# A bidirectional DeltaNet encoder layer: two products of the DeltaNet chain take float32 operands in place of float16 pairs

## The chip, the cores and the metric

The kernel runs on one core of a Trainium2 chip. The metric is device time in microseconds (us), as the median of several executions. Everything said of where the time goes comes from one profiled execution. The engines are named as in the profile: PE (TensorE) multiplies matrices, PEld is its loading of the stationary operand, DVE is VectorE, ACT is ScalarE, POOL is GpSimd and SP issues the DMA transfers.

## The reference

One layer of an encoder, applied to two requests of 4096 and 2048 tokens with shared weights, in float32. The input projection feeds three groups of heads: attention in a window of 128, a gated DeltaNet that runs over the sequence forwards and backwards, and attention on a memory of 256 tokens. Each is multiplied by a gate; one output projection and a layer norm follow. The part that the change touches is the DeltaNet's recurrence, here cut to its core (chunks of 64 tokens, 4 heads, keys and values 64 wide, one state S of 64x64 for each head):

```python
def gated_delta_chunked(q, k, v, g, beta):
    ...
    u = solve(v * beta[..., None])
    w = solve(k_beta * jnp.exp(g)[..., None])
    qk = jnp.einsum('...id,...jd->...ij', q, k) * decay
    q_dec = q * jnp.exp(g)[..., None]
    k_dec = k * jnp.exp(g[..., -1:] - g)[..., None]
    g_tot = jnp.exp(g[..., -1])

    def step(S, xs):
        u_c, w_c, qk_c, qd_c, kd_c, gt_c = xs
        v_new = u_c - jnp.einsum('...cd,...de->...ce', w_c, S)
        o_c = jnp.einsum('...cd,...de->...ce', qd_c, S) + jnp.einsum('...ij,...je->...ie', qk_c, v_new)
        S = S * gt_c[..., None, None] + jnp.einsum('...cd,...ce->...de', kd_c, v_new)
        return S, o_c
    ...

def deltanet_branch(q, k, v, a, b, conv_w, A_log, dt_bias, norm_g):
    ...
    o = gated_delta_chunked(qs, ks, vs, gs, bs)   # both directions
    o = o[0] + o[1][..., ::-1, :]
    o = o * lax.rsqrt(jnp.mean(o * o, -1, keepdims=True) + RMS_EPS) * norm_g.astype(f32)
```

## The kernel before

The tokens are cut into 48 tiles of 128 (two tiles make a pair). Where float32 accuracy is wanted from float16 products, a float32 value is held as two float16 values, high and low: `split` writes the high part on ACT and the remainder on DVE, and `mm3` multiplies two such pairs in three products (high x high, high x low, low x high).

The program has three stretches in time. In the first (to about 1300 us) every tile gets its layer norm, projections, convolution and window attention. In the second, the forward one (about 1420 to 2400 us), the DeltaNet runs forwards over the 48 tiles, and beside it PE does the projection of the gates and the memory attention (`gate_proj`: 72 products a tile, tile `psg`). In the third, the backward one (about 2400 us to the end), the DeltaNet runs backwards, and beside it PE does the output projection (`finish`: 48 products of 512 columns a tile, tiles `pso<-w2a,yT` and `pso<-w2b,yT`).

For the DeltaNet a tile goes through these steps, in either direction:

- `dn_prep` (in `dn_front`, two pairs at a time): the products of keys with keys and with queries (`psk`), times decays, give `n` (the matrix to be inverted) and `p` (what multiplies the tile's own new values; float32). `p` is split into `phl`.
- `dn_invert`: `n` goes to DRAM (`nd`) and comes back as blocks of 32 (`na`), which POOL inverts in 30 dependent steps of two operations (`tb`, `nb`) for two pairs together; the result goes out (`ud`) and comes back (`uc`).
- `dn_prep2`: the tile's values `v32`, its features `fmc`, and the keys `n32` are loaded; POOL multiplies the keys by their decay (`kc32`, shown as `kc<-n,egs`), and `kc32` is split into `kc`, each key written twice so that 128 columns are filled.
- `dn_level`: two blocks of 32 become one of 64 (`psy`, `psz`, giving `th`).
- `dn_chain`: the recurrence itself. `psr` is the product with the state's pair `shl`; then `vs` and `v` on DVE; `psx` with `th` (float32 operands, one half of the tile), a copy on ACT; `psb` with `n` (float32), an addition on DVE; `psx2` with `th` (float32, the other half), a copy on ACT. Now `v32` holds the tile's new values. They are split into `rx`; `pss` is the product of `kc` with `rx` (`mm3`, four heads) and makes the new state `sf`; its split `shl` is what the next tile waits for. `pso` is the product of the features with the old state and of `phl` with `rx` (`mm3`), the tile's outputs.

The profile calls these tiles by their program names with the numbers left out: `v32` is `v`, `psx2` is `psx`, and the products of `phl` and `rx` are `pso<-rx,phl`. Nearly all instructions are recorded by one line (L505), so tiles tell them apart.

The order of the instructions on each engine isn't that of the code: `Plan` collects all operations and puts them in order with a model of costs, several times over, and keeps the order whose modelled end is earliest. It does this once for the first stretch and once for the other two. On the chip each engine then goes through its list in that order. The plan's price of a PE product counts its columns and takes float32 fourfold:

```python
            return max(25.0, 0.4167 * n + 2.5) * (4 if mybir.dt.size(ins[0].dtype) == 4 else 1)
```

Buffers that set how far things can run ahead: `n` and `phl` hold three pairs in one pool and one pair in another (`kept_front`), `kc` and `rx` two tiles.

Of the kernel before, what the change touches and what calls it, by code (L numbers as in the profile page):

```python
# [9 lines left out]
F32 = mybir.dt.float32  # L10
# [540 lines left out]
def encoder(ctx: ExitStack, tc: tile.TileContext, A, outs):  # L551
# [315 lines left out]
    def dn_prep(pool, psp, dr, t, e, n):  # L867
# [14 lines left out]

        p = pool.tile([P, 4, P], F32, tag="p", name="p", bufs=1)
        for hp in range(2):
            hs = slice(2 * hp, 2 * hp + 2)
            psk = psp.tile([P, 2, 2, P], F32, tag="fr", name="psk", bufs=1)
            for h2 in range(2):
                h = 2 * hp + h2
                T.matmul(psk[:, :, h2], lhsT=fm[:, 2 * h + 1, :], rhs=fm[:, 2 * h:2 * h + 2, :],
                         start=True, stop=False)  # L890
                T.matmul(psk[:, :, h2], lhsT=ks[:, h, :], rhs=fm[:, 2 * h:2 * h + 2, :], start=False, stop=True)
            V.tensor_tensor(n[:, hs], psk[:, 1], e[:, hs], op=ALU.mult)
            V.scalar_tensor_tensor(p[:, hs], psk[:, 0], -(2.0 ** 10), e[:, hs], op0=ALU.mult, op1=ALU.mult)
        d["n"] = n
        phl = pool.tile([P, 2, 4, P], F16, tag="phl", name="phl", bufs=2 * PAIRS)
        split(None, phl[:, 0], phl[:, 1], p)
        d["phl"] = phl
        d["t"], d["dr"] = t, dr
        return d

    def dn_prep2(pool, d):
# [7 lines left out]
        Q.dma_start(out=n32, in_=dn_d[d["t"]])  # L909
        kc32 = pool.tile([P, 4, 64], F32, tag="kc32", name="kc32", bufs=1)  # L910
        G.tensor_tensor(kc32, n32, eg[:, 1].unsqueeze(2).to_broadcast([P, 4, 64]), op=ALU.mult)
        kc = pool.tile([P, 2, 4, 2, 64], F16, tag="kc", name="kc", bufs=2)
        split(None, kc[:, 0], kc[:, 1], kc32.unsqueeze(2).to_broadcast([P, 4, 2, 64]))
        d["kc"] = kc
# [96 lines left out]
    def dn_chain(pool, psp, dr, d):  # L1011

        sf, shl = state["f"], state["hl"]
        fm, th, kc, phl, v32, eg, n = d["fm"], d["th"], d["kc"], d["phl"], d["v"], d["eg"], d["n"]
        fa = slice(0, 64) if dr == 0 else slice(64, 128)
# [25 lines left out]
        S.activation(v32[fb], px2[fb], AF.Copy)  # L1041
        rx = pool.tile([P, 2, 4, 64], F16, tag="rx", name="rx", bufs=2)
        split(None, rx[:, 0], rx[:, 1], v32, scale=2.0 ** -7)

        pss = psp.tile([P, 512], F32, tag="ch", name="pss", bufs=1)
        ps_ = pss[:, 0:256].rearrange("p (h d) -> p h d", h=4)
        for h in range(4):
            mm3(ps_[:, h], tuple(kc[:, a, h].rearrange("p s d -> p (s d)") for a in range(2)),
                (rx[:, 0, h], rx[:, 1, h]))
        st = pool.tile([P, 4, 64], F32, tag="st_", name="st_", bufs=1)  # L1050
        G.tensor_tensor(st, sf, eg[:, 2].unsqueeze(2).to_broadcast([P, 4, 64]), op=ALU.mult)
        sf2 = pool.tile([P, 4, 64], F32, tag="sf", name="sf", bufs=2)
        V.scalar_tensor_tensor(sf2, ps_, -(2.0 ** -10), st, op0=ALU.mult, op1=ALU.add)
        shl2 = pool.tile([P, 2, 4, 64], F16, tag="shl", name="shl", bufs=2)
# [8 lines left out]
        for h in range(4):  # L1063
            mm3(po[:, 1, h], (phl[:, 0, h], phl[:, 1, h]), (rx[:, 0, h], rx[:, 1, h]))
        return po, eg[:, 0]
# [389 lines left out]
    def dn_back(pool, psp, dr, tiles, ds, emit_out):  # L1455
        for i, (t, d) in enumerate(zip(tiles, ds)):
            dn_level(pool, psp, dr, d)
            first = pos_of[t] == 0 if dr == 0 else pos_of[t] == lens[seq_of[t]] - 1
            if first:
# [4 lines left out]
             for m in range(4)]  # L1464
# [9 lines left out]
    kept_front = {"n": (pf, "n", 1), "phl": (pf, "phl", 2), "uc": (pf, "uc", 1)}  # L1474
    early = dict(kept_front, nb=(pf, "nb", 1), tb=(pf, "tb", 1), fm=(pa, "aphl", 2), ks=(pa, "oat", 2), cr=(pa, "raw", 4), p=(pa, "rawv", 2),
                 na=(gx, "x", 3))
# [111 lines left out]
    for k in range(EARLY):  # L1588
        if k % 2 == 0:
            xTe = pa.tile([P, 2, 16, P], F16, tag="xT", name="xT", bufs=2)  # L1590
        gate_proj(gorder[k], xTe[:, k % 2], pa, (("qktm", 2), ("cth", 1)))
    plan.keep([d[k] for d in fr[0] for k in ("n", "phl", "uc")])
    plan.keep([wa, wb] + [x for g in gated.values() for x in g])
# [223 lines left out]
```

## Time and profile before

| | us |
|---|---|
| median of 3 executions | 3229.03 (3227.76 to 3230.68) |
| the profiled execution, its own time | 3223.55 |
| its span, first to last instruction | 3221.8 |
| PE busy | 2833.5 (88%) |
| DVE busy | 2652.9 (82%) |
| ACT busy | 2179.3 (68%) |
| POOL busy | 1765.8 (55%) |

The span is 1.75 us shorter than that execution's own time, and that execution is 5.5 us below the median. Busy time of PE is an upper reading, since products are pipelined and a group's last one is counted to its modelled end. The kernel has no single engine that is full throughout, so shares of the whole span say little by themselves: a change has to be priced in the stretch in which it acts.

### The profile page before, as it was taken

What the parts mean: (1) busy time and instruction counts of PE and PEld (TensorE: products, weight loads), DVE (VectorE), ACT (ScalarE), POOL (GpSimd) and SP (SyncE); (2) the same over time, 40 slices, a digit from 0 to 9 for tenths busy, and PEclk for the clock granted to TensorE, in tenths of its full rate; (3) what the DMA queues carried; (4) which work ended last, traced back from release to release, by engine and by line L of the source; (5) the groups of instructions that cost most, each with busy time, mean ns of one, the idle gap of its engine ahead of it and who ended that gap; (6) DMA issues with size and microseconds to landing.
All of it is one profiled execution on the core that took longest, in us unless ns stands there. A gap on an engine that the chain in (4) does not pass through costs nothing.

```text
span 3221.8 us, 79556 instructions
## 1 busy us (share of the span) xinstructions
PE 2833.5 (88%) x28704; PEld 1889.5 (59%) x28704; DVE 2652.9 (82%) x6256; ACT 2179.3 (68%) x5623; POOL 1765.8 (55%) x2923
## 2 busy tenths in 40 slices
PE   5789887888988897778999999999998998898998
PEld 4666766667666675445565555665554554554544
DVE  8799877899999999678878787887778887887875
ACT  5677756777777776577777667776666666565543
POOL 5756444455565455535734253444538766867762
PEclk9899988999999998889999999999999999999999
DMA  7999999999999999899888887877798887777763
GB/s 220 260 228 233 221 225 229 240 236 214 228 210 226 207 227 254 206 224 197 189 182 203 188 200 160 174 175 164 159 218 209 195 189 183 190 185 178 187 170 114
DMA packets 1336900, 652.35 MB, mean 202 GB/s; under 512 B 1127728, under 2 KB 1261744, under 8 KB 1332280
## 3 DMA queue, kind: packets, MB, share of 16 engines
q1 hardware_dynamic: 1336504, 647.27, 87.5%
q8 instruction: 225, 3.69, 0.5%
q14 instruction: 171, 1.40, 0.1%
HBM read 227.54 MB, written 175.19 MB: 125 GB/s over the span
## 4 chain that ended last, share of the span: by engine, by line
PE 24%; DVE 24%; POOL 19%; DMA 13%; issue 8%; ACT 8%; SPq 3%; POOLq 0%; ACTq 0%; DVEq 0%
PE psg L505 8%; POOL nb L505 6%; POOL tb L505 5%; DVE acc L505 5%; PE pso L505 4%; PE psf L505 3%; SPq L505 3%; DMA apt<-aphl 3%; DVE lg L505 2%; DVE aphl L505 2%; PE psk L505 2%; DMA na<-nd 2%; PE psx L505 1%; ACT lg L505 1%; DMA uc<-ud 1%
## 5 line engine op out<-in xcount | busy, mean ns | idle before, releaser
L505 PEld LDWEIGHTS <-xT 128*128 128x128 f16 x5760 | 535.7, 99 | 381.4 <-issue 43.8
L505 PE MATMUL psf<-xT,w1f 128*128 128x256 f16 (+1 forms) x3600 | 443.2, 276 | 13.3 <-DVE vtm L505 7.8
L505 PE MATMUL psg<-w2a,xT 128*128 128x512 f16 (+1 forms) x2304 | 435.5, 330 | 6.4 <-DVE qtm L505 4.4
L505 PEld LDWEIGHTS <-w1f 128*128 128x128 f16 x3600 | 341.0, 101 | 56.6 <-DVE vtm L505 7.2
L505 POOL TENSOR_TENSOR nb<-nb,tb 128x30 f32<-128x30 f32 (+6 forms) x750 | 342.7, 457 | 48.7
L505 POOL TENSOR_TENSOR tb<-nb,na 128x30 f32<-128x30 f32 (+6 forms) x750 | 327.0, 436 | 48.4
L505 DVE SCALAR_TENSOR_TENSOR acc<-cb,cw,acc 128x256 f32<-128x256 f32 x576 | 326.1, 598 | 7.3 <-POOL cb L505 4.6
L505 ACT ACTIVATE lg<-lg,mx,scal 128x385 f32<-128x385 f32 (+1 forms) x384 | 263.8, 688 | 89.7 <-DVE mx L505 81.6
L505 PEld LDWEIGHTS <-yT 128*128 128x128 f16 x2304 | 201.2, 98 | 193.2 <-issue 9.9
L505 PE MATMUL pso<-w2b,yT 128*128 128x512 f16 x1152 | 297.4, 385 | 0.0
L505 PE MATMUL pso<-w2a,yT 128*128 128x512 f16 x1152 | 291.5, 381 | 1.4 <-DMA yT<-yhl 1.4
L505 PE MATMUL pslg<-kfm,qfm 128*128 128x128 f16 x2240 | 197.3, 230 | 108.3 <-DVE mx L505 105.1
L505 PEld LDWEIGHTS <-qfm 128*128 128x128 f16 x2624 | 201.4, 102 | 154.3 <-issue 127.3
L505 PE MATMUL psg<-w2b,xT 128*128 128x512 f16 x1152 | 290.2, 384 | 0.0
L505 PE MATMUL psq<-w1t,xT 128*128 128x512 f16 x1152 | 283.2, 383 | 2.5 <-ACT cb L505 2.5
L505 POOL TENSOR_TENSOR x<-x,grow 128x256 f32<-128x256 f32 x208 | 189.1, 925 | 128.9 <-ACT x L505 117.4
L505 DVE TENSOR_TENSOR aphl<-lg,aphl 128x768 f16<-128x768 f32 (+1 forms) x192 | 201.5, 1049 | 56.2 <-ACT aphl L505 56.0
L505 POOL TENSOR_TENSOR n<-raw 128x256 f32<-128x256 f16 x96 | 79.6, 840 | 245.6 <-DMA raw<-cfh 113.1
L505 DVE CUSTOM_DVE_ANT_0 lg<-pslg,bias 128x385 f32<-128x385 f32 (+1 forms) x384 | 195.2, 540 | 22.8 <-ACT oat L505 10.8
L505 POOL TENSOR_TENSOR x<-x,brow 128x256 f32<-128x256 f32 x208 | 193.9, 949 | 0.0
L505 ACT ACTIVATE aphl<-lg 128x768 f16<-128x768 f32 (+1 forms) x192 | 156.4, 815 | 17.8 <-DMA apt<-aphl 15.9
L505 PE MATMUL psk<-w1t,xT 128*128 128x272 f16 x1152 | 157.9, 284 | 9.3 <-DVE qktm L505 9.2
(921 smaller groups left out, 6865.9 us busy)
## 6 DMA issues: line engine op xcount, KB each, us to landing
x<-x SPq DMA_DIRECT2D x48, 512.0 KB, 4.0
xT<-xT SPq DMA_DIRECT2D x24, 1024.0 KB, 5.8
xT<-xT SPq DMA_DIRECT2D x48, 512.0 KB, 4.7
r<-x SPq DMA_DIRECT2D x48, 512.0 KB, 4.1
out_dram<-r SPq DMA_DIRECT2D x48, 512.0 KB, 3.7
cr<-crow SPq DMA_DIRECT2D x47, 512.0 KB, 4.8
yhl<-yhl SPq DMA_DIRECT2D x48, 384.0 KB, 3.2
x<-in_x_prompt_dram SPq DMA_DIRECT2D x32, 512.0 KB, 4.9
```

The costliest lines, as they stand in the source:

```text
L505: getattr(self.eng[o["e"]], o["name"])(*o["args"], **o["kw"])
```

## The change

Three operands of the chain stay in float32. `p` is kept as it is (its own buffers have the slots that `phl` had, of the same size) and is not split; `v32` is used as it is and not split into `rx`; the decayed keys are written by ACT in float32, straight from the loaded keys with the decay as the scale, once for each head. The products of `pss`, and those of `pso` with the tile's own values, become one float32 product a head in place of three float16 products. Scale factors follow.

```diff
-        p = pool.tile([P, 4, P], F32, tag="p", name="p", bufs=1)
+        p = pool.tile([P, 4, P], F32, tag="phl", name="p", bufs=2 * PAIRS)
...
-            V.scalar_tensor_tensor(p[:, hs], psk[:, 0], -(2.0 ** 10), e[:, hs], op0=ALU.mult, op1=ALU.mult)
+            V.scalar_tensor_tensor(p[:, hs], psk[:, 0], -(2.0 ** 3), e[:, hs], op0=ALU.mult, op1=ALU.mult)
         d["n"] = n
-        phl = pool.tile([P, 2, 4, P], F16, tag="phl", name="phl", bufs=2 * PAIRS)
-        split(None, phl[:, 0], phl[:, 1], p)
-        d["phl"] = phl
+        d["p"] = p
...
-        kc32 = pool.tile([P, 4, 64], F32, tag="kc32", name="kc32", bufs=1)
-        G.tensor_tensor(kc32, n32, eg[:, 1].unsqueeze(2).to_broadcast([P, 4, 64]), op=ALU.mult)
-        kc = pool.tile([P, 2, 4, 2, 64], F16, tag="kc", name="kc", bufs=2)
-        split(None, kc[:, 0], kc[:, 1], kc32.unsqueeze(2).to_broadcast([P, 4, 2, 64]))
+        kc = pool.tile([P, 4, 2, 64], F32, tag="kc", name="kc", bufs=2)
+        for h in range(4):
+            S.activation(kc[:, h], n32[:, h].unsqueeze(1).to_broadcast([P, 2, 64]), AF.Copy, scale=eg[:, 1, h:h + 1])
...
-        rx = pool.tile([P, 2, 4, 64], F16, tag="rx", name="rx", bufs=2)
-        split(None, rx[:, 0], rx[:, 1], v32, scale=2.0 ** -7)
...
-            mm3(ps_[:, h], tuple(kc[:, a, h].rearrange("p s d -> p (s d)") for a in range(2)),
-                (rx[:, 0, h], rx[:, 1, h]))
+            T.matmul(ps_[:, h], lhsT=kc[:, h].rearrange("p s d -> p (s d)"), rhs=v32[:, h], start=True, stop=True)
...
-        V.scalar_tensor_tensor(sf2, ps_, -(2.0 ** -10), st, op0=ALU.mult, op1=ALU.add)
+        V.scalar_tensor_tensor(sf2, ps_, -(2.0 ** -17), st, op0=ALU.mult, op1=ALU.add)
...
-            mm3(po[:, 1, h], (phl[:, 0, h], phl[:, 1, h]), (rx[:, 0, h], rx[:, 1, h]))
+            T.matmul(po[:, 1, h], lhsT=p[:, h], rhs=v32[:, h], start=True, stop=True)
```

Since the operations differ, the plan makes another order for every engine. Two places show it.

On PE, in the backward stretch, before: the first product of `phl` and `rx` of a tile (`pso`) and the first of `kc` and `rx` (`pss`), which need the high parts alone. They stand among the output projection's products (`pso_24644`); the other eleven of each, a load and a product every time, follow some rows later.

```order
L505 LDWEIGHTS phl
L505 MATMUL pso<-rx,phl 128x64
L505 LDWEIGHTS kc
L505 MATMUL pss<-rx,kc 128x64
L505 LDWEIGHTS yT
L505 MATMUL pso_24644<-w2b,yT 128x512
```

And now, at a tile of the same stretch, between the output projection's products (`pso_24610`). A float32 product stands as one row with its load inside; "x4" are the four heads.

```order
L505 LDWEIGHTS yT
L505 MATMUL pso_24610<-w2a,yT 128x512
L505 MATMUL pso<-v_24623,p 128x64 x4
L505 MATMUL pss<-v_24623,kc 128x64 x4
L505 LDWEIGHTS yT
L505 MATMUL pso_24610<-w2a,yT 128x512
```

A tile's 24 products with 24 loads became eight rows. Of its four products with `p`, those that stand ahead of its last `pss` are 2.7 on average in the backward stretch and 1.7 in the forward one; of the twelve with `phl` it had been 8.5 and 6.2.

On DVE, in the backward stretch, from the addition in the middle of a tile's chain (`v<-psb`) to its new state (`sf<-pss`), before:

```order
L505 TENSOR_TENSOR v_25326<-psb,v_25326 64x256
L505 TENSOR_TENSOR yd<-yd,oss 128x256
L505 TENSOR_SCALAR ost<-ost,scal 128x1
L505 SCALAR_TENSOR_TENSOR r<-r,ost,w2b 128x1024
L505 TENSOR_TENSOR ydh<-yd,ydh 128x256
L505 TENSOR_TENSOR phl<-p,phl 128x512
L505 TENSOR_TENSOR cr<-cr,m_ge 128x512
L505 SCALAR_TENSOR_TENSOR rx<-v_25326,rx 128x256
L505 SCALAR_TENSOR_TENSOR r<-r,ost,w2b 128x1024
L505 TENSOR_TENSOR cr<-cr,m_ge 128x512 x2
L505 TENSOR_TENSOR ytl_21532<-psy,yth_21531 32x4x32
L505 TENSOR_TENSOR of<-of,pso 128x256
```

And now, at a tile there:

```order
L505 TENSOR_TENSOR v_25090<-psb,v_25090 64x256
L505 SCALAR_TENSOR_TENSOR sf<-pss,st__25109 128x256
L505 TENSOR_TENSOR ytl_21526<-psy,yth_21525 32x4x32
L505 TENSOR_TENSOR shl<-sf,shl 128x256
L505 TENSOR_TENSOR of<-of,pso 128x256
```

`rx` and `phl` are gone from DVE's list, and here no other work was put between `v` and `sf`: DVE stands at `sf` until PE has done the last `psx` and the tile's `pss`.

## Rows read from the trace of the kernel before

**Rows 1.** The stretches: busy time of each engine in the forward one and in the backward one. Columns: the stretch and its length in us, then busy us (and count of instructions) of PE, PEld, DVE, ACT and POOL, the granted share of the TensorE clock, the DMA engines' share and GB/s.

```profile
1420.00:2400.00 980.00, 916.23 (x9380) 582.45 (x9377) 784.80 (x1851) 701.95 (x1938) 462.21 (x1005) 0.98 0.82 185
2400.00:3222.00 822.00, 738.81 (x6766) 408.12 (x6764) 642.36 (x1475) 471.46 (x1308) 565.54 (x1009) 0.98 0.75 181
```

**Rows 2.** The chain of waits that ended last: the costliest lines' shares of the forward stretch, and of the backward one.

```profile
by line: PE psg L505 24.7%; POOL nb L505 8.0%; POOL tb L505 7.1%; issue 6.3%; PE psx L505 2.8%; DMA na<-nd 2.7%; DMA fm<-dst 2.6%; SPq L505 2.5%; PE psk L505 2.5%; DMA uc<-ud 2.1%; DVE mmx L505 1.7%; DMA cr<-crow 1.7%; ACT p L505 1.7%; PE p
by line: PE pso L505 14.5%; POOL nb L505 13.7%; POOL tb L505 11.5%; issue 6.9%; SPq L505 4.2%; DMA na<-nd 4.0%; POOL oss L505 3.3%; POOL of L505 3.0%; DMA uc<-ud 2.7%; DVE r L505 2.4%; PE psx L505 2.4%; DMA cr<-crow 2.1%; POOL ost L505 1.8%
```

**Rows 3.** What PE's products waited for from 1420 us to the end, longest first in total. Columns: who waited and for whom, us in total, times, the longest in us.

```profile
PE psx L505 <- DVE v L505: 27.0, 41, 1.9
PE psy L505 <- DVE tt L505: 20.7, 11, 3.4
PE psr L505 <- DVE shl L505: 16.1, 23, 2.0
PE psy L505 <- DVE of L505: 10.6, 8, 2.1
...
PE psr L505 <- ACT shl L505: 6.2, 8, 2.0
...
PE pso L505 <- DVE rx L505: 4.3, 8, 1.2
...
PE pss L505 <- ACT rx L505: 3.6, 4, 1.7
...
PE pss L505 <- DVE rx L505: 1.8, 2, 1.0
PE pso L505 <- ACT rx L505: 1.8, 2, 1.5
PE pss L505 <- DVE kc L505: 1.7, 1, 1.7
...
PE pss L505 <- ACT kc L505: 0.8, 1, 0.8
```

**Rows 4.** Groups of products and of loads of the stationary operand, whole span. Columns: line, engine, operation, tiles, shapes (for a load rows*columns; the moving operand's shape for a product), count | busy us, mean ns of one | idle us before, and who ended it.

```profile
L505 PE MATMUL psx<-v,th 64*64 64x64 f32 x1536 | 132.3, 226 | 31.8 <-DVE v L505 27.0 <-DVE ost L505 2.2 <-ACT th L505 0.9
L505 PEld LDWEIGHTS psx<-v,th 64*64 64x64 f32 x1536 | 106.0, 136 | 101.9 <-issue 52.8 <-DVE v L505 13.8 <-ACT th L505 8.8
L505 PE MATMUL pso<-rx,phl 128*128 128x64 f16 x1152 | 64.9, 193 | 6.5 <-DVE rx L505 4.5 <-ACT rx L505 1.8
L505 PE MATMUL pss<-rx,kc 128*128 128x64 f16 x1152 | 63.5, 193 | 8.5 <-ACT rx L505 3.6 <-DVE rx L505 1.8 <-DVE kc L505 1.7
L505 PEld LDWEIGHTS <-kc 128*128 128x128 f16 x1152 | 50.3, 98 | 22.0 <-issue 4.0 <-DVE kc L505 2.3 <-ACT kc L505 1.1
L505 PEld LDWEIGHTS <-gx 128*32 128x32 f16 x24 | 1.4, 96 | 0.4
```

**Rows 5.** Two places of the timeline, the loads of a float32 group and the products of two float16 groups that follow each other. Columns: start us, us from the first's start to the last's end, engine, line, operation, tiles, shapes, count.

```profile
1906.13 0.54 PEld L505 LDWEIGHTS psx<-v,th 64*64 64x64 f32 x8 [0.32 <-issue]
...
1912.55 0.48 PE L505 MATMUL pso<-rx,phl 128*128 128x64 f16 x11
1912.87 0.48 PE L505 MATMUL pss<-rx,kc 128*128 128x64 f16 x11
```

**Rows 6.** Groups on DVE, ACT and POOL, whole span: those that go, and ACT's copy of 128 elements with a scale. Columns as in Rows 4.

```profile
L505 DVE TENSOR_TENSOR kc<-kc,kc 128x512 f16<-128x512 f32 x96 | 73.0, 760 | 5.2 <-ACT kc L505 4.8
L505 ACT ACTIVATE th<-uc,scal 128x128 f32<-128x128 f32 x192 | 72.6, 392 | 0.9
L505 DVE TENSOR_TENSOR phl<-p,phl 128x512 f16<-128x512 f32 x96 | 69.7, 726 | 11.8 <-ACT phl L505 11.0
L505 POOL TENSOR_TENSOR kc<-n,egs 128x256 f32<-128x256 f32 x96 | 63.6, 663 | 100.2 <-DVE kc L505 60.9 <-DVE p L505 19.0 <-DMA n<-dn 7.9
L505 ACT ACTIVATE kc<-kc 128x512 f16<-128x512 f32 x96 | 60.5, 630 | 21.0 <-PE pss L505 10.2 <-POOL kc L505 8.7 <-POOL nb L505 1.5
L505 ACT ACTIVATE phl<-p 128x512 f16<-128x512 f32 x96 | 60.2, 627 | 6.0 <-DVE p L505 4.4
L505 DVE SCALAR_TENSOR_TENSOR rx<-v,rx 128x256 f16<-128x256 f32 x96 | 45.2, 471 | 11.6 <-ACT rx L505 11.1
L505 ACT ACTIVATE rx<-v 128x256 f16<-128x256 f32 x96 | 39.1, 407 | 1.0
```

**Rows 7.** The end of one tile's chain in the timeline of the backward stretch. Columns as in Rows 5; in brackets the engine's idle time before and who ended it.

```profile
2816.27 0.38 ACT L505 ACTIVATE v<-psx 64x256 f32<-64x256 f32 x1
...
2816.83 0.42 ACT L505 ACTIVATE rx<-v 128x256 f16<-128x256 f32 x1
...
2817.50 0.40 DVE L505 SCALAR_TENSOR_TENSOR rx<-v,rx 128x256 f16<-128x256 f32 x1
...
2818.14 0.48 PE L505 MATMUL pso<-rx,phl 128*128 128x64 f16 x11
...
2818.47 0.48 PE L505 MATMUL pss<-rx,kc 128*128 128x64 f16 x11
...
2818.99 0.42 DVE L505 SCALAR_TENSOR_TENSOR sf<-pss,st__25199 128x256 f32<-128x256 f32 x1 [0.76 <-PE pss L505]
```

**Rows 8.** The chain of waits, shares of a hundred us of the forward stretch (1900 to 2000 us).

```profile
by line: PE psg L505 19.3%; POOL nb L505 15.8%; POOL tb L505 13.3%; DMA na<-nd 5.8%; issue 5.7%; SPq L505 4.3%; DMA uc<-ud 3.9%; PE psk L505 3.2%; PE psx L505 3.0%; POOL kc L505 2.3%; DMA ud<-nb 2.0%; PE psb L505 1.8%; PE psmo L505 1.4%; PE
```

More of the change, by code (lines that the diff above doesn't have):

```diff
@@ L1013, in dn_chain @@
         sf, shl = state["f"], state["hl"]
-        fm, th, kc, phl, v32, eg, n = d["fm"], d["th"], d["kc"], d["phl"], d["v"], d["eg"], d["n"]
+        fm, th, kc, p, v32, eg, n = (d[k] for k in ("fm", "th", "kc", "p", "v", "eg", "n"))
         fa = slice(0, 64) if dr == 0 else slice(64, 128)
@@ L1474, in encoder @@
     kept_front = {"n": (pf, "n", 1), "phl": (pf, "phl", 2), "uc": (pf, "uc", 1)}
-    early = dict(kept_front, nb=(pf, "nb", 1), tb=(pf, "tb", 1), fm=(pa, "aphl", 2), ks=(pa, "oat", 2), cr=(pa, "raw", 4), p=(pa, "rawv", 2),
+    early = dict(kept_front, nb=(pf, "nb", 1), tb=(pf, "tb", 1), fm=(pa, "aphl", 2), ks=(pa, "oat", 2), cr=(pa, "raw", 4),
                  na=(gx, "x", 3))
@@ L1591, in encoder @@
         gate_proj(gorder[k], xTe[:, k % 2], pa, (("qktm", 2), ("cth", 1)))
-    plan.keep([d[k] for d in fr[0] for k in ("n", "phl", "uc")])
+    plan.keep([d[k] for d in fr[0] for k in ("n", "p", "uc")])
     plan.keep([wa, wb] + [x for g in gated.values() for x in g])
```

## The prediction

> **What bounds the kernel now.** The change acts only where the DeltaNet's chain runs, so I first read the two stretches apart [rows 1]. In the forward stretch PE is busy for 916 of 980 us (idle 64), in the backward one for 739 of 822 (idle 83). DVE follows with 785 and 642, ACT with 702 and 471, POOL with 462 and 566. PE is the fullest engine in both, at 93% and 90%.
>
> Next, the chain of waits [rows 2]. In the forward stretch it runs through the gates' products (`psg`, 24.7%) more than through anything else; POOL's inversion (`nb` and `tb`) has 15.1%. In the backward stretch POOL's operations in the row (`nb`, `tb`, `oss`, `of`, `ost`) have 33%, and the output projection (`pso`) 14.5%. So forwards PE's amount of work sets the pace; backwards it is shared between POOL's inversion and PE.
>
> Last, what PE waits for in its 147 us of idle time [rows 3]: results of DVE that belong to the chain, above all (`v` 27.0, `tt` 20.7, `shl` 16.1, `of` 10.6). The operands that go in this change account for 4.3 + 3.6 + 1.8 + 1.8 + 1.7 + 0.8 = 14.0 us.
>
> **PE.** A tile now has 12 + 12 float16 products for `pss` and `pso`, 1152 of each in all [rows 4]. In a row they follow each other every 0.029 us: eleven of `pso` take the 0.32 us from 1912.55 to 1912.87 [rows 5]. That is 24 x 0.029 = 0.70 us a tile.
>
> After it there are eight float32 products. The chip runs a float32 product in two passes: the code has 8 `psx` products a tile, 768 for 96 tiles and directions, and the trace has 1536 of them and 1536 loads [rows 4]. So 16 passes a tile. What a pass takes for a load of 128 columns no row shows, since the float32 operands of now have 64. Eight loads of that kind take 0.54 us, one 0.136 [rows 4, 5], so a pass comes every (0.54 - 0.136) / 7 = 0.058 us.
>
> The bounds: if columns don't matter to a load, 0.058 (float16 loads of 128 and of 32 columns take 98 and 96 ns [rows 4]); if the pass is as long as its load and that grows with the columns, 0.116. A float32 load of 64 columns takes 136 ns, longer than the 98 of a float16 load of 128, so float32 operands evidently load in another, slower way, and I place the value near the upper end, at 0.11: 16 x 0.11 = 1.76 us. PE's work grows by 1.06 us a tile, 102 us over 96 (bounds 0.23 x 96 = 22 and 1.16 x 96 = 111).
>
> The Trainium skill speaks against the change here: its page "TensorE: Matmul & The Clock Gate" says in "Weight-path perf modes — Fast Weight Load (FWL) and DoubleRow" that the fast load works for 128 columns and not for float32, and in "LDWEIGHTS (loading the stationary operand)" that a load takes its columns divided by 1.2 ns. By that rule a pass would be 107 ns and PE's added work, as an estimate, 16 x 0.107 - 0.70 = 1.01 us a tile, 97 us in all; by the rows' lower bound 22. For 64 columns the rule gives 53 ns, which the trace's 58 ns a pass agrees with; for 128 no run here shows it yet.
>
> The plan prices a float32 product of 64 columns at 4 x 29.2 = 117 ns, two passes of 58. If they take 110, PE runs 0.8 us a tile behind its plan, and what waits for `pss` or `pso` is late by that.
>
> **The other engines.** DVE loses the three remainders: 73.0 + 69.7 + 45.2 = 188 us [rows 6], nearly all in the two stretches, 13% of its 785 + 642 there. POOL loses the keys' decay, 63.6 us. ACT loses 60.5 + 60.2 + 39.1 = 160 us and gets four copies with a scale a tile; the nearest row (`th<-uc`, 128 elements, with a scale) has 392 ns, so 4 x 96 x 0.392 = 151 us: nothing gained, and one more thing in front of the chain's copies where the plan puts it there. The DMAs stay as they are. The buffers stay too: `p` has the slots of `phl`.
>
> **The chain's own length.** From the last copy of `v` (ends 2816.65) to `sf` (starts 2818.99) a tile takes 2.34 us now, through both halves of the split and eleven products of each kind [rows 7]. Afterwards it is a hand-off to PE, which I take as 0.2 us (from that copy's end to the split's start it is 0.18 here), perhaps 0.2 of a product under way, and 0.88 us for `pss`, about 1.4 with the drain; but with `p`'s four products ahead of `pss`, as the order has it for two thirds of them backwards and 42% forwards, up to 2.3. So the chain gets shorter by 0 to 0.9 us a tile, less than the removed split suggests, because the float32 passes take most of it back.
>
> **The sum.** PE's list gets 102 us longer; the question is how much of its 147 us of waiting goes. (a) The 14 us for `rx` and `kc` go. (b) Its four longest waits for DVE, 74 us in total [rows 3], shrink with a DVE that has 13% less to do; since such waits fall faster than load, I take a third, 25 us (bounds 10, by 13%, and 37, by half). (c) The waits for `shl`, 16.1 + 6.2 = 22.3 us, come right behind `pss`; where `pss` stands first, `p`'s products fill that time. Half: 11 us. (d) POOL's decay of the keys is on the chain of waits itself, 2.3% of a hundred us [rows 8]; over the stretches' 1802 us that would be 41. Half of it again, since the inversion's other waits stay: 20 us. Together 70 of 147.
>
> 102 - 70 = +32 us, against that execution's own 3223.55 us: 3255.6. The median lies 5.5 us above it, so 3261 us. The first stretch I leave as it is: it loses two tiles' splits of `p`, about 3 us of work beside 1300 us of other work, and its order changes throughout, which may move it by some us either way.
>
> **The rivals.**
>
> *PE's work is hidden and the backward stretch gets faster.* Its place is the backward stretch, its mechanism POOL's inversion, which holds a third of the chain there [rows 2]. Half of POOL's 63.6 us lies in it, 32 us; if that and 10 us of DVE waits come off the chain while PE's 51 us fit into its 83 idle ones, the stretch falls by 42. Forwards, 51 us meet only 64 idle ones [rows 1], and with half of (a) to (d) off, 16 remain. Together -26: 3203 us. It decides from the point where the backward stretch falls by more than the forward one rises. For it: POOL's share; against it: PE is at 90% there too.
>
> *A float32 load of 128 columns costs no more than one of 64.* Then PE's work grows by 22 us, and with the same 70 off it is -48: 3181 us. Against it is the 136 ns load.
>
> *PE's waits stay.* They belong to the chain's order, and the plan, which prices the passes too low, may put its waits elsewhere. Then only (a) is gained: 102 - 14 = +88, 3317 us.
>
> *Nothing to be measured.* Less than 0.2% either way, about 6.5 us, is what a measurement of this kernel can't tell from no change; the relief of DVE and POOL would just pay for the passes (3229 us).
>
> **How the numbers follow.** The forecast, about +7 to +65 us, gets 0.51; the waits that stay 0.12; nothing 0.11; the faster backward stretch 0.21; the cheap load 0.05. So slower 0.63, the same 0.11, faster 0.26. The range takes half of the faster backward stretch's cases and most of the staying waits': 3200 to 3313 us.
>
> **What would show it.** In the profile after: 1536 passes and loads each for `pss` and for `pso<-v,p`, and the stretch of eight passes, about 0.11 x 7 + 0.24 = 1.0 us against 0.48 for eleven now; with 0.058 it would be 0.65, and the load's duration would tell the same (some 190 ns against 136). DVE's busy time falls by about 188 us, POOL's by 64, ACT's by less than 20. PE's idle time in the two stretches falls from 147 to about 80 us and the stretches together grow by about 30, the forward one more than the backward. The prediction is wrong if the float32 passes come every 0.06 us, or if PE's idle time shrinks by more than 100 us, or if the first stretch moves by more than 10 us, which nothing in the sum provides for.

## The result

The changed kernel takes 3251.36 us (median; 3243.70 to 3255.10), beside 3228.40 for the kernel before on the same chip: a ratio of 1.0069, 95% interval 1.0047 to 1.0091, so 15 to 29 us slower. The profiled execution took 3248.76 us, with a span of 3247.0. The forecast had the median at 3261 us, +32; the sign is right, and the change costs +22. How much of the reasoning holds is what the experiments are about.

The stretches of the changed kernel, with the columns of [rows 1]:

```profile
1420.00:2400.00 980.00, 947.08 (x8941) 630.12 (x8940) 690.31 (x1679) 687.03 (x1963) 407.36 (x965) 0.99 0.80 182
2400.00:3247.00 847.00, 794.82 (x6534) 471.85 (x6532) 579.85 (x1376) 477.64 (x1396) 507.48 (x959) 0.98 0.75 180
```

PE is idle for 33 + 52 = 85 us now, where it was idle for 147 [rows 1], and busy for 87 us longer. DVE has 157 us less work in the two stretches and POOL 113, far more than its 64 us of decayed keys; what the rest is, the last section says.

The two new groups of products, their loads, and ACT's keys; columns as in [rows 4]:

```profile
L505 PE MATMUL pss<-v,kc 128*128 128x64 f32 x768 | 100.8, 272 | 0.2 <-ACT v L505 0.2
L505 PEld LDWEIGHTS pss<-v,kc 128*128 128x128 f32 x768 | 98.6, 193 | 6.6 <-ACT v L505 0.7
L505 ACT ACTIVATE kc<-n,egs 128x128 f32<-128x128 f32 x384 | 132.5, 394 | 36.9 <-PE pss L505 31.2 <-DMA n<-dn 4.5 <-issue 0.5
```

A load takes 193 ns on average, and 768 records are 384 products in two passes. The end of one tile's chain, to be held against [rows 7]:

```profile
2834.97 0.38 ACT L505 ACTIVATE v<-psx 64x256 f32<-64x256 f32 x1
...
2835.39 0.97 PEld L505 LDWEIGHTS pss<-v,kc 128*128 128x128 f32 x8 [0.71 <-ACT v L505]
2835.40 1.10 PE L505 MATMUL pss<-v,kc 128*128 128x64 f32 x8 [0.22 <-ACT v L505]
...
2836.34 1.06 PE L505 MATMUL pso<-v,p 128*128 128x64 f32 x8
...
2836.54 0.42 DVE L505 SCALAR_TENSOR_TENSOR sf<-pss,st__24971 128x256 f32<-128x256 f32 x1 [1.00 <-PE pss L505]
```

Eight passes take 2836.34 - 2835.40 = 0.94 us, and from the copy's end (2835.35) to `sf` it is 1.19 us, where the tile in [rows 7] took 2.34. That is one tile of each; over all 96 the median from the last copy to `sf` falls from 3.06 to 2.32 us. The chain did get shorter, and yet the kernel got slower.

PE's longest waits after, to be held against [rows 3]:

```profile
PE psx L505 <- DVE v L505: 13.2, 18, 2.9
PE psy L505 <- DVE tt L505: 12.6, 8, 3.3
PE psk L505 <- DVE p L505: 10.0, 9, 2.1
PE psr L505 <- DVE shl L505: 9.3, 14, 2.1
...
PE psr L505 <- ACT shl L505: 3.3, 6, 1.7
...
PE psy L505 <- DVE of L505: 0.8, 2, 0.4
```

The four waits for DVE that the forecast counted on (`v`, `tt`, `shl`, `of`) fell from 74.4 to 35.9 us. That looks like the forecast's term (b). Whether a lighter DVE did it isn't to be seen in a profile that changed in everything at once.

### The profile page after: what moved, and what is told of

Read it like the earlier page. It is cut to its first block, busy times and chain, and to the rows that moved or that the text cites. A ratio compares the mean times of both kernels' runs of the same rounds, so it can differ in the third digit from the quotient of the medians.

```text
span 3247.0 us, 77749 instructions
## 1 busy us (share of the span) xinstructions
PE 2914.7 (90%) x27936; PEld 1996.5 (61%) x27936; DVE 2488.3 (77%) x5968; ACT 2159.1 (66%) x5719; POOL 1657.8 (51%) x2827
## 5 line engine op out<-in xcount | busy, mean ns | idle before, releaser
L505 PE MATMUL psg<-w2a,xT 128*128 128x512 f16 (+1 forms) x2304 | 443.6, 330 | 4.2 <-DVE qtm L505 2.9
L505 POOL TENSOR_TENSOR nb<-nb,tb 128x30 f32<-128x30 f32 (+6 forms) x750 | 319.3, 426 | 49.7
L505 POOL TENSOR_TENSOR tb<-nb,na 128x30 f32<-128x30 f32 (+6 forms) x750 | 306.9, 409 | 50.3
L505 POOL TENSOR_TENSOR x<-x,grow 128x256 f32<-128x256 f32 x208 | 182.2, 892 | 144.3 <-ACT x L505 135.5
L505 PE MATMUL psov<-vtm,apt 128*128 128x64 f16 x3360 | 135.4, 196 | 46.1 <-DMA apt<-aphl 43.0
L505 PEld LDWEIGHTS <-apt 128*128 128x128 f16 x3360 | 125.6, 100 | 68.9 <-DMA apt<-aphl 56.1
```

Source lines behind the costliest of these rows:

```text
L505: getattr(self.eng[o["e"]], o["name"])(*o["args"], **o["kw"])
```

## Experiments

The theory is the forecast's: PE's added work comes whole, and a lighter DVE and POOL give some waits back. The rivals: PE's work is taken in by PE's own waits; or the new order of the instructions makes the difference. Ratios are to the kernel before on the same chip, with their 95% interval; a thousandth is 3.2 us. Where a run keeps every instruction at its place, the plan is given the old price for what was changed (those lines are left out below), and DVE, ACT and POOL go through the same lists as in the kernel that the run is held against.

### Less PE work after the change: 64 columns of `p`

```
-            T.matmul(po[:, 1, h], lhsT=p[:, h], rhs=v32[:, h], start=True, stop=True)
+            T.matmul(po[0:64, 1, h], lhsT=p[:, h, 0:64], rhs=v32[:, h], start=True, stop=True)
...
```

(DVE's two additions of this product take half the partitions)

> The changed kernel, with every instruction at its place, but the product of `p` with `v` loads only 64 of `p`'s 128 columns (the tile's own part of the output is left out for half of its tokens). In 8 of the 16 passes a tile the load then has the 64 columns that take 0.058 us a pass in the rows of before, where the trace after has 0.112: 8 x 0.054 x 96 = 41 us less work for PE, and not one operation less on another engine (DVE's additions have the same shape of half the partitions). Theory (the passes of 128 columns are what the change costs, and PE's amount of work sets the pace): 25 to 41 us below the changed kernel, 3210 to 3226 us. Rival (the new order of the work, or other waits, makes the difference, and PE's passes fill time in which it would wait): within 6 us of the changed kernel, 3245 to 3257 us.

3252.67 us, ratio 1.0059 (1.0038 to 1.0080): with the changed kernel's 1.0069 a difference of -3 us, uncertain by 10. The rival's number. The timeline of this run shows that the work did fall, though by far less than 41 us:

```profile
2424.92 0.68 PE L505 MATMUL pso<-v,p 128*64 128x64 f32 x8
...
2425.53 1.10 PE L505 MATMUL pss<-v,kc 128*128 128x64 f32 x8
...
2426.47 1.24 PE L505 MATMUL pso<-w2a,yT 128*128 128x512 f16 x5
```

The eight shorter passes take 0.61 us, the eight others 0.94 as in the changed kernel: 0.33 a tile, 32 us in all. That includes what PE pays for going on from loads of 64 columns to loads of 128; going over to 64 costs another 95 ns or so each time (last section), which leaves some 20 us less work. By the theory these should have shown as about 20 us; measured are 3, uncertain by 10, so they were worth less than that, but the test is weaker than was planned.

### Less DVE work before the change

```
-        split(None, rx[:, 0], rx[:, 1], v32, scale=2.0 ** -7)
+        S.activation(rx[:, 0], v32, AF.Copy, scale=2.0 ** -7)
...
+        V.scalar_tensor_tensor(rx[:, 1, 0], v32[:, 0], 2.0 ** -7, rx[:, 0, 0], op0=ALU.mult, op1=ALU.subtract)
...
-                (rx[:, 0, h], rx[:, 1, h]))
+                (rx[:, 0, h], rx[:, 1, 0]))
```

(and likewise for `phl` and `kc`)

> The kernel before, with every instruction at its place, but DVE makes the three remainders (of `kc`, `phl` and `rx`) for one head in four, and PE uses that one for all heads (the low parts of the other heads are left out). DVE has about 130 us less to do, PE, ACT and POOL the same. Theory (a lighter DVE shortens PE's waits, the terms (a) and (b) of the sum, and the chain): 15 to 35 us below the kernel before, 3193 to 3213 us, with PE's idle time in the two stretches falling from 147 by about the same. Rival (PE's own work is the bound and the relief of DVE is worth next to nothing, so that the saved waits come from somewhere else): 3220 to 3235 us.

3196.40 us, ratio 0.9888 (0.9859 to 0.9918): -36 us (-27 to -46), the theory's number. The stretches, in one row from 1420 us to the end, of the kernel before and of this one:

```profile
1420.00:3221.80 1801.80, 1655.04 (x16145) 990.57 (x16141) 1427.16 (x3326) 1173.41 (x3245) 1027.75 (x2013) 0.98 0.79 183
```

```profile
1420.00:3196.60 1776.60, 1652.45 (x16189) 993.38 (x16187) 1343.56 (x3330) 1173.06 (x3250) 982.24 (x2017) 0.98 0.80 186
```

DVE has 84 us less here (90 in the whole span, where 130 were expected), and PE's idle time falls from 146.8 to 124.2, its four waits for DVE from 74.4 to 50.6. POOL's busy time falls by 45 us although not one of its instructions changed. So the -36 us are not the price of DVE's work alone: POOL's shorter operations are in it, and so is the remainder of `rx` in the chain itself (284 ns on average, where it was 471).

### More DVE and POOL work after the change

```
+        V.tensor_tensor(pd, p, ks, op=ALU.subtract)
...
+        G.tensor_tensor(kc32, n32, eg[:, 1].unsqueeze(2).to_broadcast([P, 4, 64]), op=ALU.mult)
...
+        V.tensor_tensor(kd, kc32.unsqueeze(2).to_broadcast([P, 4, 2, 64]), d["fm"][:, 0:4].rearrange("p h (s d) -> p h s d", s=2), op=ALU.subtract)
...
+        V.scalar_tensor_tensor(rx, v32, 2.0 ** -7, fm[:, 0:4, 0:64], op0=ALU.mult, op1=ALU.subtract)
```

> The changed kernel, with DVE's three remainders (nothing reads them) and POOL's decay of the keys put back: DVE +188, POOL +64 us, PE and ACT as in the changed kernel; the plan orders it anew. Theory (the 60 to 80 us of PE's waits that the change won back came from DVE and POOL): 40 to 70 us above the changed kernel, 3290 to 3320 us, with the idle time of PE in the two stretches back at 125 to 155 us. Rival (PE, now busy for 95% of the stretches, hides them): 3245 to 3262 us.

3270.55 us, ratio 1.0118 (1.0089 to 1.0148): 16 us above the changed kernel, uncertain by some 12. Neither number, and PE's idle time is 108.5 us, between 85 and the 125 to 155 of the theory: the relief that the change gave is worth something, but well under the 40 to 70 us that the theory had.

```profile
1420.00:3268.10 1848.10, 1739.58 (x15379) 1093.77 (x15376) 1430.38 (x3325) 1155.40 (x3343) 1027.76 (x2018) 0.98 0.76 179
```

Two things differ from the run with less DVE work, though: the plan ordered this kernel anew, and nothing waits for the remainders here.

### Another price in the plan

```
-            return max(25.0, 0.4167 * n + 2.5) * (4 if mybir.dt.size(ins[0].dtype) == 4 else 1)
+            if mybir.dt.size(ins[0].dtype) == 4:
+                return 2.0 * max(58.0, 0.875 * self.free(ins[0]))
+            return max(25.0, 0.4167 * n + 2.5)
```

> The changed kernel, but the plan prices a float32 product by what its two passes take, 2 x 0.112 us for 128 columns and 2 x 0.058 for 64, where the changed kernel has 4 x 29.2 ns for both; the same instructions in another order. Theory (the price matters little, since PE works off its list anyway and its waits are mostly gone): 3240 to 3258 us. Rival (the plan lets PE run 0.8 us a tile behind, and what waits for it pays): 3230 us or less.

3301.12 us, ratio 1.0215 (1.0182 to 1.0248): 47 us above the changed kernel, which neither expected. The same instructions, planned with the passes' true duration, run slower. So an order alone can cost more than the change does.

### More PE work before the change

```
-            mm3(ps_[:, h], tuple(kc[:, a, h].rearrange("p s d -> p (s d)") for a in range(2)),
-                (rx[:, 0, h], rx[:, 1, h]))
+            mm3(pss[:, 64 * h:64 * (h + 3)].rearrange("p (k d) -> p k d", k=3),
+                tuple(kc[:, a, h].rearrange("p s d -> p (s d)") for a in range(2)),
+                tuple(rx[:, a, h].unsqueeze(1).to_broadcast([P, 3, 64]) for a in range(2)))
...
-            mm3(po[:, 1, h], (phl[:, 0, h], phl[:, 1, h]), (rx[:, 0, h], rx[:, 1, h]))
+            mm3(po[:, 1, h:4], (phl[:, 0, h], phl[:, 1, h]),
+                tuple(rx[:, a, h].unsqueeze(1).to_broadcast([P, 4 - h, 64]) for a in range(2)))
```

> The kernel before, with every instruction at its place on every engine, but the 24 float16 products of `pss` and `pso` a tile move more columns (192 each for `pss`, 256, 192, 128 and 64 for the four heads of `pso`; the surplus columns land where the next head's product overwrites them). By 1/2.4 ns a column, as the products of 512 columns in the trace show it (379 ns with their fill), PE gets 0.64 + 0.48 = 1.12 us more a tile, 107 us in all, which is what the float32 passes of the change cost (my 102), and no engine is relieved. Theory (in the forecast's sum PE's 102 us come whole and only a lighter DVE and POOL give waits back): 80 to 107 us above the kernel before, 3309 to 3336 us. Rival (PE's waits, 147 us in the two stretches, take a large part of the work in by themselves): 3250 to 3290 us, PE's idle time in the stretches then below 100 us.

3251.37 us, ratio 1.0064 (1.0040 to 1.0088): +21 us (+13 to +28) for 107 us of PE work. That is the rival, at the lower end of its range. The same row of this kernel, and then its longest waits of PE:

```profile
1420.00:3245.30 1825.30, 1737.25 (x16154) 1088.73 (x16150) 1429.31 (x3325) 1179.25 (x3245) 1034.07 (x2013) 0.99 0.77 181
```

```profile
PE psx L508 <- DVE v L508: 17.1, 31, 1.9
PE psy L508 <- DVE tt L508: 8.2, 8, 1.8
PE psr L508 <- DVE shl L508: 7.7, 17, 1.0
PE psy L508 <- DVE of L508: 6.1, 8, 1.1
```

PE's idle time is 88 us, nearly what the change left (85), and the four waits for DVE are down from 74.4 to 39.1 us, with DVE exactly as loaded as before (1429 us). While PE works longer, what it would have waited for gets ready. PE's added work alone is enough for the drop that I had put down to the lighter DVE.

PE's busy time grew by 82 us, not by 107. The granted clock is 0.99 in this row, where it was 0.98: by the trace's records PE ran at 1.2 GHz, the lower of its two levels, for 62 us of the two stretches before and for 24 here. Over whole executions the share is 0.963 to 0.970 here, 0.954 to 0.963 in the kernel before on the same chip. A clock that falls less often while PE has more to do is thus part of why the added work cost so little; as an estimate, 38 us less at half the speed save up to 19 us.

### The PE work of the change taken away

```
+        top = lambda x: x.bitcast(mybir.dt.bfloat16).rearrange("p (c two) -> p c two", two=2)[:, :, 1]
...
-            T.matmul(po[:, 1, h], lhsT=p[:, h], rhs=v32[:, h], start=True, stop=True)
+            T.matmul(po[:, 1, h], lhsT=top(p[:, h]), rhs=top(v32[:, h]), start=True, stop=True)
```

(and likewise for `pss`)

> The changed kernel, with every instruction at its place, but the eight float32 products a tile read only the upper halves of `kc`, `p` and `v` as bfloat16 (the lower 16 bits are left out): one pass each in place of two of 0.112 us. If a load of every second bfloat16 takes no longer than a float16 load (98 ns, hidden in part), PE has 1.2 to 1.5 us a tile less, 115 to 145 us in all; the other engines and the waits of every instruction are the same. Theory (PE's passes set the pace, and its waits come back in part): 55 to 110 us below the changed kernel, 3141 to 3196 us. Rival (after the change the chain and its order set the pace, not PE's work, as the 64-column loads hint): 3235 to 3257 us.

3224.23 us, ratio 0.9981 (0.9967 to 0.9995): 28 us below the changed kernel, between the two expectations. These products follow each other every 30 ns, so PE has 16 x 0.112 - 8 x 0.030 = 1.55 us a tile less, 149 us in all; again a microsecond of PE's work is worth 0.2. PE's idle time goes from 85 to 168 us, and the granted clock falls to 0.97 (96 us at 1.2 GHz, against 57 in the changed kernel):

```profile
1420.00:3222.80 1802.80, 1634.96 (x14692) 955.34 (x14689) 1268.66 (x3052) 1156.82 (x3353) 918.66 (x1923) 0.97 0.78 184
```

### What another order does

```
-    LAT = {"PE": 200.0, "DVE": 150.0, "ACT": 170.0, "POOL": 40.0, "SP": 0.0}
+    LAT = {"PE": 200.0, "DVE": 151.0, "ACT": 170.0, "POOL": 40.0, "SP": 0.0}
```

> The kernel before with the same instructions, ordered anew by a plan that takes DVE's latency as 151 instead of 150 ns. It shows what the order alone does. If an order is worth little: within 10 us of the kernel before, 3219 to 3239 us. If the difference of 22 us that was measured may be luck of the order: more than 15 us away, either side.

> The changed kernel with the same instructions, ordered anew by a plan that takes DVE's latency as 151 instead of 150 ns. If an order is worth little: within 10 us of the changed kernel, 3241 to 3261 us, and 15 to 30 us above the kernel before in its own second order. If the measured 22 us are luck of the order: more than 15 us away, either side.

The kernel before in its second order: 3231.03 us, ratio 0.9990 (0.9976 to 1.0004). The changed one in its second: 3240.43 us, ratio 1.0024 (1.0009 to 1.0038), so +8 us where the first order has +22: some 14 us less, uncertain by 9, and so between the two expectations. Slower it is in both, but by how much depends on luck of the order. The gain comes from the first stretch: the first state update (`sf`) starts at 1403.5 us in this order, at 1425.4 in the changed kernel's own, and at 1420.9 and 1417.3 in the two orders of the kernel before; what follows takes 1831.1 us, against 1821.6, 1800.9 and 1802.5 in the other three. In the stretches where the change acts it costs 20 to 30 us in either order. The first state update of the changed kernel, in its own order and in the second:

```profile
L505 DVE SCALAR_TENSOR_TENSOR sf<-pss,st__21584 x1: 425/425/425, 1425.4 to 1425.4; 128x256 f32<-128x256 f32 x1
```

```profile
L505 DVE SCALAR_TENSOR_TENSOR sf<-pss,st__21584 x1: 423/423/423, 1403.5 to 1403.5; 128x256 f32<-128x256 f32 x1
```

### Both edits of the kernel before at once

The diff is those of the second and the fifth experiment together.

> The kernel before, every instruction at its place, with both edits at once: PE's products of `pss` and `pso` with more columns (PE +107 us, alone +21) and DVE's three remainders for one head in four (DVE -90 us in the trace, alone -36; the low parts of the other heads are left out). Theory 1 (each engine's work has a price of its own, and they add up): 3230 + 21 - 36, that is 3207 to 3223 us. Theory 2 (with PE fuller a lighter DVE is worth little, which would explain why the change gains nothing from its lighter DVE and POOL): 3238 to 3255 us.

3220.19 us, ratio 0.9962 (0.9949 to 0.9976): -12 us, where the sum of the two gives -15. Theory 1: the prices add up, and a lighter DVE is worth as much with a full PE (-33) as without (-36).

```profile
1420.00:3221.50 1801.50, 1730.06 (x16191) 1088.35 (x16189) 1345.23 (x3331) 1183.88 (x3250) 992.64 (x2018) 1.00 0.79 183
```

This makes it a riddle why the change loses time. The changed kernel has about the same PE work as this one, and 75 us less on DVE and 78 less on POOL; yet its two stretches are 25 us longer (1827.0 against 1801.5), and PE waits 14 us longer in them. The other 12 us are PE's busy time, 1741.9 against 1730.1 for about the same work: the granted clock is 1.00 in the row above (11 us at 1.2 GHz), 0.99 and 0.98 in the changed kernel's (57 us).

### The change in halves

Only the state update; the diff is to the changed kernel, and puts the outputs' float16 pairs back:

```
+        phl = pool.tile([P, 2, 4, P], F16, tag="phl", name="phl", bufs=2 * PAIRS)
+        split(None, phl[:, 0], phl[:, 1], p)
...
+        split(None, rx[:, 0], rx[:, 1], v32, scale=2.0 ** -7)
...
-            T.matmul(po[:, 1, h], lhsT=p[:, h], rhs=v32[:, h], start=True, stop=True)
+            mm3(po[:, 1, h], (phl[:, 0, h], phl[:, 1, h]), (rx[:, 0, h], rx[:, 1, h]))
```

> One half of the change: the state update `pss` in float32 with `kc` from ScalarE, while the tile's own outputs stay with the float16 splits of `p` and `v`. PE +51, DVE -73 (of `kc`), POOL -64 us; `rx` and `phl` stay. At the prices per microsecond that the experiments so far give (PE 0.2, DVE 0.4 where PE is not full): +10 - 29 and something for POOL, 3195 to 3215 us. If relief is worth little once PE gets more work: 3232 to 3250 us.

Only the tile's own outputs; to the changed kernel again:

```
+        G.tensor_tensor(kc32, n32, eg[:, 1].unsqueeze(2).to_broadcast([P, 4, 64]), op=ALU.mult)
...
+        split(None, kc[:, 0], kc[:, 1], kc32.unsqueeze(2).to_broadcast([P, 4, 2, 64]))
...
+        split(None, rx[:, 0], rx[:, 1], v32, scale=2.0 ** -7)
...
-            T.matmul(ps_[:, h], lhsT=kc[:, h].rearrange("p s d -> p (s d)"), rhs=v32[:, h], start=True, stop=True)
+            mm3(ps_[:, h], tuple(kc[:, a, h].rearrange("p s d -> p (s d)") for a in range(2)),
+                (rx[:, 0, h], rx[:, 1, h]))
```

> The other half: the tile's own outputs in float32 from `p` and `v`, while `pss` keeps the float16 splits of `kc` and `rx`. PE +51, DVE -70, ACT -60 us; POOL and the chain's `rx` as before. At the prices so far: +10 - 28, 3205 to 3220 us. If relief is worth little once PE gets more work: 3235 to 3255 us.

The state update alone: 3227.11 us, ratio 0.9980 (0.9966 to 0.9994), -6 us, between the two expectations. The outputs alone: 3248.51 us, ratio 1.0045 (1.0029 to 1.0061), +15 us, as if relief were worth little. So the prices found in the order of before don't carry over to programs that the plan orders anew. In the outputs' half the first state update starts 14 us later than in the kernel before (1434.6 against 1420.9), which is half of the 27 us that separate the two profiled executions (the medians differ by 15): again the order of the first stretch, in which this half changes next to no work. The halves sum up to +9 us, about what the changed kernel shows in its second order.

### No remainders at all

```
-        split(None, phl[:, 0], phl[:, 1], p)
...
-        split(None, rx[:, 0], rx[:, 1], v32, scale=2.0 ** -7)
+        S.activation(rx, v32, AF.Copy, scale=2.0 ** -7)
...
-            mm3(po[:, 1, h], (phl[:, 0, h], phl[:, 1, h]), (rx[:, 0, h], rx[:, 1, h]))
+            T.matmul(po[:, 1, h], lhsT=p[:, h], rhs=rx[:, h], start=True, stop=True)
```

(and likewise for `kc` and `pss`)

> The kernel before without the low parts: `kc`, `p` and `v` are rounded to float16 and each head has one product for `pss` and one for `pso` (the remainders and their products are left out, `p` is written in float16 at once). DVE -188, PE -16 x 0.029 x 96 = -45, ACT -60 us, POOL as before; the plan orders it anew. With the prices so far (DVE 0.4, PE 0.2): -75 - 9, 3140 to 3160 us. If DVE's relief is worth only what lies on the chain itself (the remainder of `rx`, 0.3 to 0.5 us a tile, and the eleven products, 0.3): 3155 to 3190 us. If the order counts for more than either: 3190 us and up.

3176.04 us, ratio 0.9826 (0.9807 to 0.9845): -56 us, faster than both kernels, at float16's accuracy in these two products. That is in the range of the second expectation, by which relief counts for what lies on the chain; the order may have its part. It has the PE work of the run with upper halves and the same DVE (1276 against 1269 us), more POOL (984 against 919) and 28 us less ACT, and is 48 us faster. What sets the two apart is the order, planned for what runs here and for products of 117 ns there, and the way `kc` and `rx` are made: by POOL and one copy of ACT each here, by ACT's four copies and not at all there.

## Why the prediction was right, and where it was not

**PE's added work: right.** The row of eight passes lasts 1.10 us (forecast 1.0), passes follow each other every 0.112 us (median; forecast 0.11), and a load takes 193 ns (190): 16 x 0.112 - 0.70 = 1.09 us a tile, 105 us (102). By this the rival of the cheap load is out. The rule of the Trainium skill (page "TensorE: Matmul & The Clock Gate", section "LDWEIGHTS (loading the stationary operand)") gave 107 ns a pass, and the trace agrees within 5%; the load's own record is longer, 193 ns. Wrong was the count among the signs: there are 768 passes for `pss` and as many for `pso<-v,p`, 1536 together; the sum had the right 16 a tile. DVE's busy time fell by 165 us in the whole span (forecast 188), POOL's by 108 (64) and ACT's by 20 (less than 20).

**PE's idle time: right in size (85 us, forecast 80), wrong in cause.** The failed step is "102 - 70" as a sum of a cost that comes whole and of waits that a lighter DVE and POOL give back. With 107 us more work and no relief at all PE's idle time falls just as far, from 147 to 88. PE's work costs 0.2 us per us, in either kernel's order (+21 for 107, -28 for 149; the -3 for 20 doesn't speak against it). PE is the fullest engine at 93% and 90% [rows 1] and still its amount of work doesn't set the pace. So the term was about 20 us, not 102. Two more things in the 70 don't hold: the 16.1 us for `shl` stand in (b) and again in (c), about 5 us twice, and (d) is POOL's time on the chain of waits, taken off PE's idle time.

**(a) to (c):** the waits went, but PE's added work alone is enough for that. What a lighter DVE is worth in the kernel before is about what (b) said, in PE's idle time (-23 us), and more in the time (-36). The chain from the last copy to `sf` got shorter by 0.74 us in the median, within the forecast's 0 to 0.9.

**(d) POOL's decay of the keys: not seen in the time.** What POOL waited for from 1420 us on, before and after:

```profile
POOL nb L505 <- DMA na<-nd: 130.9, 37, 18.3
POOL kc L505 <- DVE kc L505: 60.9, 22, 8.8
POOL ost L505 <- DVE ost L505: 57.5, 17, 9.4
```

```profile
POOL nb L505 <- DMA na<-nd: 174.0, 40, 13.4
...
POOL ost L505 <- DVE ost L505: 122.5, 21, 11.3
```

Two waits grew by 43 + 65 = 108 us, and the 60.9 us for `kc` are gone. In all POOL is idle for 138 us more in the stretches, its 113 us less of work and the 25 us by which they got longer. The 2.3% of the chain of waits [rows 8] don't show up as a gain: POOL waits longer instead, for the blocks of the next inversion (`na`) and for DVE (`ost`). What the decay alone is worth no run shows.

**Where +22 us come from.** In the order of before, PE's 107 us more and DVE's 90 us less were worth -12 together, and the change takes off nearly twice as much on DVE. It lost 22 us, or 8 in its second order. So the forecast had PE's cost five times too high; it took 70 us off for the relief, where 33 to 36 were measured for about half of DVE's; and it lacked a loss of 20 to 35 us. That these come out near the measured number together is luck.

The traces show where much of the loss sits. The chain runs through four tiles, whose inverses (`th`) are made together, and then needs the inverses of the next four. From the 49th state update on there are 47 steps from one update's start to the next. The 36 inside the groups of four take 472 us now and took 546: the shorter chain gains 74 us. The 11 that lead into a new group take 349 us and took 265. In ten of these 11 the first copy of `v` starts within 1.5 us of the last copy to `th`, so the chain is waiting for the inverse, as it was before at these steps. With both edits in the order of before (the riddle above) it is 534 and 266 us, 800 together, against 821 now. One group after the change, and the same group before it: the first `n`, the last `sf` of the group two ahead, the last `th`, and the chain's first product with it.

```profile
2717.34 1.06 PE L505 MATMUL pso<-v,p 128*128 128x64 f32 x8
2717.54 0.42 DVE L505 SCALAR_TENSOR_TENSOR sf<-pss,st__24754 128x256 f32<-128x256 f32 x1 [0.16 <-PE pss L505]
...
2718.23 0.27 PE L505 MATMUL psk<-fm,ks 128*128 128x256 f16 x1
...
2718.54 0.42 DVE L505 TENSOR_TENSOR n<-psk,cr 128x256 f32<-128x256 f32 x1 [0.58 <-PE psk L505]
...
2815.19 0.56 ACT L505 ACTIVATE th<-psz 32x128 f32<-32x128 f32 x2 [1.05 <-PE psz L505]
...
2815.70 0.68 PE L505 MATMUL psx<-v,th 64*64 64x64 f32 x8
```

```profile
2690.86 0.42 DVE L505 TENSOR_TENSOR n<-psk,cr 128x256 f32<-128x256 f32 x1 [2.89 <-PE psk L505]
...
2712.16 0.42 DVE L505 SCALAR_TENSOR_TENSOR sf<-pss,st__24966 128x256 f32<-128x256 f32 x1
...
2795.16 0.56 ACT L505 ACTIVATE th<-psz 32x128 f32<-32x128 f32 x2 [1.11 <-PE psz L505]
...
2795.87 0.67 PE L505 MATMUL psx<-v,th 64*64 64x64 f32 x8
```

From the first `n` to `th` it is about 100 us in both (97 and 105 here). But before, `n` was begun 22 us ahead of the end of that older group's chain (mean of the last ten groups), and now 8; here PE's list has the product that the first `n` waits for (`psk`) behind the older group's last `pso`. What the chain gains it gives back in waiting for an inverse that is begun late. These pauses go with the order and not with an engine's load: the 11 steps take 265 to 271 us in the order of before, also with more work for PE or less for DVE, and 340 to 350 in the changed kernel's, also with less work for PE. In its second order they take 327, with the other price 320. The run without remainders shows that a shorter chain needn't be paid back like this: 498 us inside the groups, 279 between them.

That the changed instructions in the order of before would be faster isn't shown; it wasn't tried. Nor is it shown why the plan arrives at such an order, nor what ACT's four copies for `kc` cost by themselves. The forward stretch's 11 us were not split up like this.

**The rivals.** "PE hidden and the backward stretch faster" was half right: PE's work is largely hidden, but the backward stretch, from the 49th state update to the end, took 829 us instead of 820, and the forward one, from the first to the 49th, 992 instead of 981. "PE's waits stay" is out, and so is "nothing to be measured" (+0.5 to +0.9%). The first stretch kept within the 10 us (+4.5), but other orders move it by -17 to +14, which should have widened the range.

## What to carry to other kernels

How full an engine is doesn't tell what its work costs. Here 93% busy meant 0.2 us per us (0.1 to 0.3), and taking work off the engine at 80% brought 0.4 (0.3 to 0.5), with what went along on POOL and in the chain; the price of an engine's work comes from adding and taking away work with every instruction at its place. Where a planner orders the program, take two or three orders of the same instructions before a difference of under 1% is put down to the change. And if waits fall after a change that adds work to the waiting engine, that work alone may have filled them. Last, a chain that gets shorter gains nothing if it then waits longer for its next input: the steps from one state update to the next, one by one, show it.

## What the runs showed of the hardware

**DVE slows POOL's operations.** In the run with the lighter DVE, POOL has the same instructions as before; the two groups of the inversion, before and then there (the last two numbers ahead of the idle time: busy us and mean ns):

```profile
L505 POOL TENSOR_TENSOR nb<-nb,tb 128x30 f32<-128x30 f32 (+6 forms) x750 | 342.7, 457 | 48.7
L505 POOL TENSOR_TENSOR tb<-nb,na 128x30 f32<-128x30 f32 (+6 forms) x750 | 327.0, 436 | 48.4
```

```profile
L508 POOL TENSOR_TENSOR nb<-nb,tb 128x30 f32<-128x30 f32 (+6 forms) x750 | 323.5, 431 | 48.7
L508 POOL TENSOR_TENSOR tb<-nb,na 128x30 f32<-128x30 f32 (+6 forms) x750 | 312.6, 417 | 48.4
```

They got shorter by 34 us for 90 us that DVE lost; in the changed kernel they have 319.3 and 306.9 us busy. With both edits POOL is busy for 41 us less than with more PE work alone (1034.07 and 992.64 in the rows above). So part of DVE's price may be paid in POOL's time. The Trainium skill (page "SBUF — State Buffer", section "Who interferes with whom") says that a DVE instruction with two SBUF inputs contends with a POOL instruction that reads SBUF, over a port that they share; the remainders have two such inputs, and the trace agrees.

**A change of the load's width costs PE time.** In the run with 64 columns of `p`, the last of the eight passes is followed by the next product after 154 ns (median of the pairs that end such a group) instead of 58, and going from `pss` (128 columns) over to 64 takes 205 ns instead of 112: some 95 ns each way. The `psx` products of the kernel before, with loads of 64 rows and columns, show the same: 151 ns behind the last of a group, 58 between the others. The Trainium skill (page "TensorEngine Tiling (Array Packing)", section "Key Properties") says that changing the tiling mode drains the engine, which fits; that the drain is the cause no run here shows.
